# Low weight parts and row arithmetic of a two-layer encoder trunk moved from GpSimd to VectorE

## The chip, the cores and the metric

The kernel runs on one core of a Trainium2 chip. A core has five engines that work beside each other, each through its own queue in order: TensorE (PE: matmuls, and PEld: its weight loads), VectorE (DVE), ScalarE (ACT), GpSimd (POOL) and SyncE (SP, which only issues DMAs here). GpSimd and ScalarE issue some DMAs too. The metric is the device time of one launch in microseconds (us).

## The reference, cut to what matters

The input is 1024 rows of 1024 features; 16 learned rows are put in front, so 1040 rows run through two layers, and the last 1024 come out.

```
def hybrid_mixer(h, ...):                       # h: normalised rows
    proj = h @ w_in
    qkv, z, b_raw, a_raw, sc_b, sc_c, sc_h = split(proj)
    qkv = silu(depthwise_conv_centred(qkv, conv_qkv_w))
    q, k, v = split(qkv); q = l2norm(q); k = l2norm(k)
    ...
    o_fwd = chunk_gated_delta_rule(q, k, v, g[0], beta[0])
    o_bwd = flip(chunk_gated_delta_rule(flip(q), flip(k), flip(v), flip(g[1]), flip(beta[1])))
    o = o_fwd + o_bwd
    o = o * rsqrt(mean(o * o) + RMS_EPS) * dn_norm_w * silu(z)
    y_sc = sc_b * depthwise_conv_centred(sc_c * sc_h, sc_conv_w)
    return concatenate([o, y_sc]) @ w_out

for l in range(2):
    h = h + hybrid_mixer(rmsnorm(h, norm1_w[l]), ...)
    h = h + (silu(gate) * up) @ w_down          # gate, up = split(rmsnorm(h, norm2_w[l]) @ w_gate_up)
return rmsnorm(h, final_norm_w)[16:]
```

Four heads of width 128 go through the gated delta rule, in chunks, forwards and backwards; four groups of 128 channels go through the short gated convolution (sc). All is float32.

## The kernel before, in words

**Precision.** Activations lie transposed: features on the 128 partitions, the 1040 rows along the free dimension. Each float32 matrix is split into a high part, rounded to the matmul's format, and a low part, the rest; a product is three matmuls: high by high (line 157), high by low of the activations (158), low of the weights by high (159). So each 128x512 block of weights that arrives needs a DMA (129), a rounding copy on ACT (130, `whi`) and a subtraction (131, `wlo`). That is `wsplit`, called by `wload`, which gives a tile of weights in two such blocks. `whi` and `wlo` have three buffers each. The flag `lov` chooses the engine of the subtraction: DVE where it is set (the input projection's tiles from the fifth to the end of v, and the first two tiles of the list below), GpSimd elsewhere: the first four tiles of the layer, the rest of the mixer's weights, `w_out`, and the last layer's last weights (`last_weights`). The feed-forward's own weights go through another function (lines 997 and 998), with ACT and DVE.

**Mixer of a layer.** The input projection runs tile by tile, 128 output features each: `dense` does the matmuls of a chunk of rows into a PSUM bank and reads it out on DVE (line 296 by `rstd`, 720 by a row, 905 added to the residual). First k and q (with convolution, lengths, and the chunk matrices, lines 449 to 461), then a substitution of 31 steps for each direction on DVE (lines 523 and 525), then v; then a list of eight tiles: four of z (`z_tile`) and four groups of the short convolution (`sc_tile`). `z_tile` takes silu on ACT and scales the row by a column of `dn_norm_w` (line 671). `sc_tile` takes three projections: the first is multiplied by `rstd` again (716), the second by that at its read-out (720), then the convolution (309, 310), and the product with the third (729; for the last group 732 and a read-out).

**Scan and end of the mixer.** The chunks' scan (`scan_step`) runs forwards and backwards side by side; its steps alternate between PE, ACT and DVE (lines 792 to 845), and dense matmuls of z, sc and of the sc half of `w_out` are set between them. The second direction that reaches a chunk calls `finalize`: it loads the other direction's output `od` (856), subtracts `qs` (857), adds the PSUM result (858), takes the norm (864 to 868), transposes and multiplies by silu(z) (871). Then `O` is split into parts for the output projection (928 high on ACT, 929 low): 16 pieces, of which the pieces of the first quarter of the rows are on DVE and the other 12 on GpSimd. `out_part(0, m)` and then `out_part(1, m)` do the attention half of the output projection for the inner and the outer quarters of the rows, eight tiles each, and behind them the operands of the feed-forward are made (178, 950, 965, 977, 1078), the hand-off to it.

**Feed-forward and end.** Gate, up and down projections run with combined operands (lines 1015 to 1017 and 1435 to 1437). At the end the rows are scaled and stored by `scaled` (1465) on DVE or GpSimd.

**Order.** The order on each queue isn't written out: a scheduler places instructions by priority (`tc.cur_priority`, set by `at_prio`) and by an estimate of when each can run, and then each engine goes through its list. A change of one operation's engine can so move others. In the changed kernel as built, GpSimd's list has 135 rows where it had 318, VectorE's 2910 where it had 2725 (equal neighbours taken together), and the three other lists hold the same work in partly another order.

GpSimd also issues DMAs (`qdma`): the lengths of k and q (412, 415, 608, 611, 612), and it makes the 4-partition inverse of the first 16 rows (474, 475).

Of the kernel before, what the change touches and what calls it, by code (L numbers as in the profile page):

```python
# [7 lines left out]
F32 = mybir.dt.float32  # L8
# [3 lines left out]
ALU = mybir.AluOpType  # L12
# [5 lines left out]
L = 1040  # L18
# [12 lines left out]
P_N1, P_N2, P_CV, P_SC, P_DN = 0, 8, 16, 52, 64  # L31
# [11 lines left out]
def trunk(ctx: ExitStack, tc: tile.TileContext, xT, w_in, w_ba, w_out, w_gu, w_dn,  # L43
          par_d, alog_d, dtb_d, cst_d, eye_d, out):
    nc = tc.nc
# [6 lines left out]
    def nm(p):  # L52
        cnt[0] += 1
        return f"{p}_{cnt[0]}"
# [16 lines left out]
    def pa():  # L71
        return bank("a")
# [27 lines left out]
    tt = nc.vector.tensor_tensor  # L100
    stt = nc.vector.scalar_tensor_tensor
    ts = nc.vector.tensor_scalar
    ptt = nc.gpsimd.tensor_tensor
# [18 lines left out]
    lov = [False]  # L122

    def wsplit(src, hi, lo, raw=None):

        kk = src.shape[1]
        if raw is None:
            raw = wp.tile([128, WK, 128], F32, tag="raw", bufs=2, name=nm("raw"))
        dma(raw[:, 0:kk, :], src)
        whi_done[0] = act(out=hi, in_=raw[:, 0:kk, :], func=AF.Copy)  # L130
        (tt if lov[0] else ptt)(out=lo, in0=raw[:, 0:kk, :], in1=hi.bitcast(F32), op=ALU.subtract)  # L131

    def wload(src, nk):

# [145 lines left out]
    for l in range(DEPTH):  # L280
        last = l == DEPTH - 1
        X, Y = S[l % 2], S[1 - l % 2]
        pcol = lambda c: par[:, l * P_L + c:l * P_L + c + 1]
        rstd = ss
        base = tc.cur_priority

        o0 = 16 if last else 0
# [339 lines left out]
        for pos, i in enumerate(seq):  # L627
# [5 lines left out]
            t = trow()  # L633
# [32 lines left out]
        def z_tile(m):  # L666
            t = trow()
            inproj(12 + m, to_row(t), chunks=ochunks)
            t = t[:, o0:L]
            act(out=t, in_=t, func=AF.Silu)  # L670
            nc.gpsimd.tensor_scalar(out=t, in0=t, scalar1=pcol(P_DN), scalar2=1.0, op0=ALU.mult, op1=ALU.mult)
            dma(szd[m][:, o0:L], t)


# [28 lines left out]
        for i in range(4):  # L703
            t = trow()
# [8 lines left out]
        def sc_tile(i):  # L713
            t0 = trow()
            inproj(16 + 3 * i, to_row(t0))
            ptt(out=t0, in0=t0, in1=rstd, op=ALU.mult)

            def times(t):
                def f(ps, n0, n1):
                    tt(out=t[:, n0:n1], in0=ps, in1=t[:, n0:n1], op=ALU.mult)  # L720
                return f

            inproj(17 + 3 * i, times(t0))
            t2 = trow()
            conv(t0, t2, P_SC + 3 * i)
            if i < 3:
                t1 = trow()
                inproj(18 + 3 * i, to_row(t1), chunks=ochunks)
                ptt(out=t2[:, o0:L], in0=t2[:, o0:L], in1=t1[:, o0:L], op=ALU.mult)
                dma(yd[i][:, o0:L], t2[:, o0:L])  # L730
            else:
                ptt(out=t2, in0=t2, in1=rstd, op=ALU.mult)
                inproj(18 + 3 * i, times(t2), chunks=ochunks)
            return t2

# [20 lines left out]
        O = QT  # L756
# [92 lines left out]
        def finalize(c, n, s0, pof, qs, sz):  # L849

            ob = fin[:, 512 * (nfin[0] % 2):512 * (nfin[0] % 2) + 512]
            nfin[0] += 1
            o = ob[0:n].rearrange("p (h e) -> p h e", h=4)
            dma(sz, szd[:, :, s0:s0 + n].rearrange("m p t -> p m t"))
            if c > 0:
                dma(ob[0:n], od[c])
                ptt(out=o, in0=o, in1=qs[0:n], op=ALU.subtract)
                tt(out=ob[0:n], in0=pof, in1=ob[0:n], op=ALU.add)
            else:
                tt(out=ob[0:n], in0=pof, in1=qs[0:n].rearrange("p h e -> p (h e)"), op=ALU.subtract)  # L860
            pt = v4(pa())
            st = sb.tile([128, 4], F32, tag="st", bufs=2, name=nm("st"))
            for h in range(H):
                act(out=pt[0:n, h, :], in_=o[:, h, :], func=AF.Square, accum_out=st[0:n, h:h + 1])
            stt(out=st[0:n], in0=st[0:n], scalar=1.0 / HD, in1=g[0:n, 0, c, :], op0=ALU.mult, op1=ALU.add)
            act(out=st[0:n], in_=st[0:n], func=AF.Sqrt)
            nc.vector.reciprocal(out=st[0:n], in_=st[0:n])
            tt(out=o, in0=o, in1=st[0:n].unsqueeze(2).to_broadcast([n, 4, 128]), op=ALU.mult)
            for h in range(H):
                nc.tensor.transpose(pt[:, h, 0:n], o[:, h, :], ident[0:n, 0:n])  # L870
            tt(out=O[:, :, s0:s0 + n], in0=pt[:, :, 0:n], in1=sz, op=ALU.mult)
# [17 lines left out]
        t0 = o0  # L889
        yh = big(X[0][2], F32R)  # L890
        ys, yt = [], []
        for i in range(4):
            t = trow() if i < 2 else hb[1][:, i, :] if i < 3 else y3
# [26 lines left out]
        oh, ol = (sb.tile([128, 4, L], F32R, tag=f"P{d}", name=nm("o")) for d in range(2))  # L920
# [5 lines left out]
        for (n0, n1) in hcut[0] + hcut[1]:  # L926
            for h in range(H):
                act(out=oh[:, h, n0:n1], in_=O[:, h, n0:n1], func=AF.Copy)
                (tt if n0 == o0 else ptt)(out=ol[:, h, n0:n1], in0=O[:, h, n0:n1], in1=oh[:, h, n0:n1].bitcast(F32), op=ALU.subtract)
        os_ = [(oh[:, h, :], ol[:, h, :]) for h in range(H)]  # L930

        def half(ap, z):
# [478 lines left out]
        for u, (p, b, m) in enumerate(UNITS):  # L1411
# [16 lines left out]
            for j in range(NJ):  # L1428
# [9 lines left out]
                if b == NBK - 1:  # L1438
                    dh, z, op = TO[p]
                    h = part(hr[4 * dh + m], z, j)  # L1440
# [10 lines left out]
        else:  # L1451
# [22 lines left out]
            for (n0, n1) in FIN:  # L1474
# [8 lines left out]
                for m in range(KT):  # L1483
                    h = hr[m][:, n0:n1]
# [93 lines left out]
```

## Time and profile before

| | |
|---|---|
| median of 3 runs | 2513.88 us (2511.24 to 2517.37) |
| the profiled execution | 2517.22 us |
| its span, first to last instruction | 2515.4 us |
| granted TensorE clock, mean | 0.997 |
| busy: PE, DVE, ACT, POOL | 2478.2, 1696.9, 1045.9, 340.0 us |

How to read the profile's lines. In the page, each engine has its busy time, share of the span and number of instructions; the strips show the span in 40 slices, each digit a busy share in tenths. A row of a group is: source line, engine, operation, output<-inputs, shapes and count, then busy time in us and the mean of one in ns, then the engine's idle time before these instructions and what ended most of it. A row of waits is: who waits, for whom, total us, times, longest. A row of a stretch is: from:to, its length, busy time of PE, PEld, DVE, ACT and POOL with counts, granted clock, DMA share, GB/s. A row of the timeline is: start, duration, engine, line, operation, and in brackets the idle time before it and what ended it. The name `a`, `b`, `a3f` and the like are those of shared buffers.

### The profile page before, as it was taken

How to read it: one execution, taken by the hardware profiler on the slowest of the kernel's cores; microseconds unless marked ns; L12 is line 12 of the kernel's file. 1: busy time of each engine (PE TensorE's matmuls, PEld its weight loads, DVE VectorE, ACT ScalarE, POOL GpSimd, SP SyncE). 2: the span in 40 equal slices, each digit the busy share in tenths (PEclk: the TensorE clock that was granted, in tenths of full speed). 3: DMA queues.
4: the chain of work that ended last, by engine and by line, in shares of the span. 5: the costliest groups of instructions: out<-in, count | busy, mean ns of one | idle time of the engine just before them, and what ended most of it. 6: DMA issues, size and time to landing. Idle time of an engine off the chain costs nothing. (4 is left out here: it accounts for less than half of the span.)

```text
span 2515.4 us, 44862 instructions
## 1 busy us (share of the span) xinstructions
PE 2478.2 (99%) x17508; PEld 2276.9 (91%) x17508; DVE 1696.9 (67%) x3073; ACT 1045.9 (42%) x1944; POOL 340.0 (14%) x359
## 2 busy tenths in 40 slices
PE   8999999999999999999999999999999999999998
PEld 6989999999999999999999888998977888887887
DVE  4788333649877777877657893336698777677765
ACT  5554333535333333344445543335453333234444
POOL 1031212331000000000111212133400000000012
PEclk9999999999999999999999999999999999999999
DMA  3444353624323332764224443446332233238541
GB/s 127 135 166 149 112 161 130 212 77 136 116 102 102 108 102 81 256 198 133 92 77 145 152 154 116 143 131 205 120 126 101 97 105 117 90 112 279 177 120 68
DMA packets 199530, 335.27 MB, mean 133 GB/s; under 512 B 23404, under 2 KB 85668, under 8 KB 199316
## 3 DMA queue, kind: packets, MB, share of 16 engines
q1 hardware_dynamic: 171204, 293.84, 35.3%
q10 hardware_dynamic: 25936, 34.19, 4.2%
q0 software_dynamic: 2176, 4.36, 0.6%
q8 instruction: 138, 2.26, 0.4%
q14 instruction: 76, 0.62, 0.1%
HBM read 250.31 MB, written 81.99 MB: 132 GB/s over the span
## 5 line engine op out<-in xcount | busy, mean ns | idle before, releaser
L131 POOL TENSOR_TENSOR wlo<-raw,whi 128x512 fp32r<-128x512 f32 x132 | 176.4, 1338 | 1285.4 <-ACT whi L130 1116.7
L157 PE MATMUL pacc<-a,whi 128*128 128x346 f32 (+1 forms) x808 | 263.6, 329 | 8.8 <-ACT whi L130 7.6
L159 PE MATMUL pacc<-a,wlo 128*128 128x346 f32 (+1 forms) x808 | 262.4, 326 | 0.7 <-DVE wlo L131 0.5
L157 PE MATMUL pacc<-b,whi 128*128 128x346 f32 (+2 forms) x672 | 234.0, 349 | 2.4 <-ACT b L900 1.8
L159 PE MATMUL pacc<-b,wlo 128*128 128x346 f32 (+2 forms) x672 | 233.1, 348 | 0.8 <-DVE wlo L131 0.8
L158 PE MATMUL pacc<-a,whi 128*128 128x346 f32 (+1 forms) x688 | 225.1, 327 | 0.0
L130 ACT ACTIVATE whi<-raw 128x512 fp32r<-128x512 f32 x168 | 106.0, 631 | 228.3 <-PE pacc L158 124.9
L158 PE MATMUL pacc<-b,whi 128*128 128x346 f32 (+2 forms) x580 | 200.8, 346 | 0.0
L157 PEld LDWEIGHTS pacc<-a,whi 128*128 128x128 f32 x808 | 152.2, 189 | 14.6 <-ACT whi L130 8.1
L159 PEld LDWEIGHTS pacc<-a,wlo 128*128 128x128 f32 x808 | 152.9, 189 | 1.7 <-DVE wlo L131 0.8
L157 PEld LDWEIGHTS pacc<-b,whi 128*128 128x128 f32 x672 | 126.9, 189 | 14.5 <-issue 3.1
L159 PEld LDWEIGHTS pacc<-b,wlo 128*128 128x128 f32 x672 | 126.6, 189 | 9.8 <-DVE wlo L131 1.1
L158 PEld LDWEIGHTS pacc<-a,whi 128*128 128x128 f32 x688 | 130.3, 189 | 2.6 <-issue 2.1
L997 ACT ACTIVATE whi<-rw 128x512 fp32r<-128x512 f32 x92 | 57.6, 631 | 140.1 <-PE pf L1016 36.4
L158 PEld LDWEIGHTS pacc<-b,whi 128*128 128x128 f32 x580 | 109.5, 189 | 6.9 <-issue 0.4
L997 ACT ACTIVATE b<-rw 128x512 fp32r<-128x512 f32 x64 | 39.9, 631 | 135.0 <-PE pacc L1016 37.4
L296 DVE TENSOR_TENSOR a<-pacc,rstd 128x346 f32<-128x346 f32 (+2 forms) x59 | 32.7, 555 | 89.6 <-PE pacc L159 89.5
L296 DVE TENSOR_TENSOR b<-pacc,rstd 128x346 f32<-128x346 f32 (+1 forms) x63 | 32.5, 516 | 82.8 <-PE pacc L159 82.8
L131 POOL TENSOR_TENSOR a<-raw,a 128x512 fp32r<-128x512 f32 x3 | 3.9, 1285 | 597.1 <-ACT a L130 597.1
L997 ACT ACTIVATE a<-rw 128x512 fp32r<-128x512 f32 x64 | 40.0, 629 | 101.7 <-PE pacc L1016 60.3
L998 DVE TENSOR_TENSOR wlo<-rw,whi 128x512 fp32r<-128x512 f32 x92 | 62.8, 686 | 4.8 <-ACT whi L997 4.1
L1015 PE MATMUL pacc<-b,whi 128*128 128x260 f32 (+1 forms) x172 | 53.5, 311 | 0.7 <-ACT b L1051 0.7
(966 smaller groups left out, 8012.8 us busy)
## 6 DMA issues: line engine op xcount, KB each, us to landing
raw<-in_w_in SPq DMA_DIRECT2D x112, 256.0 KB, 2.5
raw<-in_w_gu SPq DMA_DIRECT2D x104, 256.0 KB, 2.9
rw<-in_w_gu SPq DMA_DIRECT2D x88, 256.0 KB, 3.0
rw<-in_w_dn SPq DMA_DIRECT2D x94, 192.0 KB, 2.7
rec<-vkd SPq DMA_DIRECT2D x61, 256.0 KB, 2.7
raw<-in_w_out SPq DMA_DIRECT2D x48, 256.0 KB, 2.8
b<-ad SPq DMA_DIRECT2D x45, 260.0 KB, 3.3
a<-ad SPq DMA_DIRECT2D x45, 256.0 KB, 5.2
```

Of the source, the lines that this page charges most:

```text
L130: whi_done[0] = act(out=hi, in_=raw[:, 0:kk, :], func=AF.Copy)
L131: (tt if lov[0] else ptt)(out=lo, in0=raw[:, 0:kk, :], in1=hi.bitcast(F32), op=ALU.subtract)
L157: mm(ps[:, :n], wh, xh[:, n0:n1], start=(k == 0), stop=False)
L158: mm(ps[:, :n], wh, xl[:, n0:n1], start=False, stop=False)
L159: mm(ps[:, :n], wl, xh[:, n0:n1], start=False, stop=(k == K - 1))
L296: tt(out=t[:, n0:n1], in0=ps, in1=rstd[:, n0:n1], op=ALU.mult)
L997: act(out=hi, in_=src, func=AF.Copy)
L998: tt(out=lo, in0=src, in1=hi.bitcast(F32), op=ALU.subtract)
L1015: mm(ps[:, :CW], w[0][:, k, :], th[:, cs], start=first and k == 0, stop=False, skip_group_check=True)
```

## The change

The low weight parts (131), the scaling of z (671), the row products of the short convolution (716, 729, 732), the subtraction in `finalize` (857) and the low parts of `O` (929) all go to VectorE. GpSimd keeps its DMA issues, the 4-partition inverse and its share of the last products (1465).

```
@@ wsplit
-        (tt if lov[0] else ptt)(out=lo, in0=raw[:, 0:kk, :], in1=hi.bitcast(F32), op=ALU.subtract)
+        tt(out=lo, in0=raw[:, 0:kk, :], in1=hi.bitcast(F32), op=ALU.subtract)
@@ z_tile
-            nc.gpsimd.tensor_scalar(out=t, in0=t, scalar1=pcol(P_DN), scalar2=1.0, op0=ALU.mult, op1=ALU.mult)
+            ts(out=t, in0=t, scalar1=pcol(P_DN), scalar2=None, op0=ALU.mult)
@@ sc_tile
-            ptt(out=t0, in0=t0, in1=rstd, op=ALU.mult)
+            tt(out=t0, in0=t0, in1=rstd, op=ALU.mult)
...
-                ptt(out=t2[:, o0:L], in0=t2[:, o0:L], in1=t1[:, o0:L], op=ALU.mult)
+                tt(out=t2[:, o0:L], in0=t2[:, o0:L], in1=t1[:, o0:L], op=ALU.mult)
...
-                ptt(out=t2, in0=t2, in1=rstd, op=ALU.mult)
+                tt(out=t2, in0=t2, in1=rstd, op=ALU.mult)
@@ finalize
-                ptt(out=o, in0=o, in1=qs[0:n], op=ALU.subtract)
+                tt(out=o, in0=o, in1=qs[0:n], op=ALU.subtract)
@@ low parts of O
-                (tt if n0 == o0 else ptt)(out=ol[:, h, n0:n1], in0=O[:, h, n0:n1], in1=oh[:, h, n0:n1].bitcast(F32), op=ALU.subtract)
+                tt(out=ol[:, h, n0:n1], in0=O[:, h, n0:n1], in1=oh[:, h, n0:n1].bitcast(F32), op=ALU.subtract)
```

## The prediction

> **What bounds the kernel now.** I read the page first: the engines' busy shares and the strips of 40 slices.
>
> ```profile
> span 2515.4 us, 44862 instructions
> ...
> PE 2478.2 (99%) x17508; PEld 2276.9 (91%) x17508; DVE 1696.9 (67%) x3073; ACT 1045.9 (42%) x1944; POOL 340.0 (14%) x359
> ...
> DVE  4788333649877777877657893336698777677765
> POOL 1031212331000000000111212133400000000012
> ```
>
> TensorE (PE) is busy for 2478.2 us of 2515.4. All that any change of VectorE (DVE) and GpSimd (POOL) work can give back is the 37.2 us in which PE idles. The strips say where the two engines meet: POOL has work in slices 0 to 9 and 19 to 28 (the mixers of the two layers) and at the very end, and DVE there runs from 3 tenths (slices 4 to 6) to 9.
>
> The waits come next, first those of all engines and then those of PE.
>
> ```profile
> POOL wlo L131 <- ACT whi L130: 1116.7, 98, 614.6
> ...
> ACT whi L130 <- PE pacc L158: 124.9, 59, 8.6
> ```
>
> ```profile
> PE pacc L157 <- ACT whi L130: 8.7, 5, 5.9
> ...
> PE pacc L159 <- DVE wlo L131: 1.4, 2, 0.8
> ```
>
> Columns: total us, times, longest. POOL waits for ScalarE (ACT), ACT waits for PE to release the weight buffers, and PE waits for a low weight part only twice, 1.4 us together, both of them parts that DVE makes already. No low part made by POOL is waited for: POOL's slowness as such is hidden.
>
> Last, busy time in the stretches that matter (PE, PEld, DVE, ACT, POOL in this order):
>
> ```profile
> 0.00:10.00 10.00, 2.88 (x7) 1.99 (x8) 3.14 (x7) 5.46 (x8) 2.70 (x6) 1.00 0.77 247
> 90.00:260.00 170.00, 166.62 (x1461) 159.15 (x1460) 147.98 (x313) 87.56 (x117) 41.47 (x88) 1.00 0.53 174
> 260.00:450.00 190.00, 190.00 (x1684) 186.73 (x1683) 60.19 (x153) 67.94 (x173) 44.14 (x31) 1.00 0.40 130
> 577.00:615.00 38.00, 35.27 (x289) 34.60 (x288) 36.78 (x56) 20.91 (x37) 6.35 (x5) 1.00 0.39 127
> 1350.00:1530.00 180.00, 177.67 (x1464) 162.85 (x1463) 153.79 (x309) 87.86 (x116) 33.31 (x60) 1.00 0.51 168
> 1720.00:1740.00 20.00, 17.95 (x92) 15.04 (x92) 14.30 (x25) 12.77 (x40) 7.36 (x5) 0.91 0.75 269
> 1740.00:1800.00 60.00, 60.00 (x341) 51.79 (x340) 29.82 (x62) 21.98 (x73) 23.97 (x25) 1.00 0.33 110
> 1800.00:1823.00 23.00, 23.00 (x196) 23.00 (x195) 18.26 (x34) 14.33 (x23) 11.10 (x9) 1.00 0.56 186
> 1823.00:1860.00 37.00, 34.20 (x210) 29.26 (x209) 36.34 (x55) 20.34 (x32) 6.17 (x4) 0.95 0.38 124
> 2500.00:2515.40 15.40, 6.89 (x68) 6.22 (x67) 6.86 (x15) 5.21 (x13) 7.52 (x10) 0.83 0.41 138
> ```
>
> PE's idle time: 7.1 us in the first 10, 8.5 after 2500; of the 21.6 left, 3.4 and 2.3 lie in the stretches of substitution (90 to 260, 1350 to 1530), 2.1 in 1720 to 1740, and 2.7 and 2.8 in the two hand-offs from mixer to feed-forward (577 to 615, 1823 to 1860), where DVE is 97 and 98% busy. Those hand-offs are DVE's; the scan (260 to 450, and to 1800 in the second layer) has DVE half idle.
>
> **What moves.** These groups of POOL work go to DVE; the rows are line, operation, shape, count | busy, mean ns.
>
> ```profile
> L131 POOL TENSOR_TENSOR wlo<-raw,whi 128x512 fp32r<-128x512 f32 x132 | 176.4, 1338 | 1285.4 <-ACT whi L130 1116.7 <-PE pacc L158 41.9 <-DMA raw<-in_w_in 38.8
> ...
> L857 POOL TENSOR_TENSOR b3f<-b3f,qs 128x512 f32<-128x512 f32 x8 | 10.3, 1296 | 39.1 <-DMA b3f<-od 24.6 <-ACT pa L864 6.9 <-PE pacc L158 5.7
> L716 POOL TENSOR_TENSOR b<-b,rstd 128x1040 f32<-128x1040 f32 x4 | 9.8, 2439 | 4.8 <-DVE b L296 3.3 <-PE pb L485 1.5
> ...
> L929 POOL TENSOR_TENSOR o<-b,o 128x260 fp32r<-128x260 f32 x12 | 9.6, 832 | 6.7 <-PE pb L807 6.7
> ```
>
> And this is what such shapes cost on DVE, and what DVE pays now when POOL runs beside it:
>
> ```profile
> L131 DVE TENSOR_TENSOR wlo<-raw,whi 128x512 fp32r<-128x512 f32 x36 | 24.7, 686 | 1.9 <-ACT whi L130 1.6
> ...
> L1356 DVE TENSOR_TENSOR a<-a,rstd 128x1040 f32<-128x1040 f32 x21 | 26.1, 1241 | 0.6
> ...
> L178 DVE SCALAR_TENSOR_TENSOR b<-a,par,b 128x346 fp32r<-128x346 f32 x14 | 12.2, 873 | 4.9 <-ACT b L177 4.9
> ...
> L865 DVE SCALAR_TENSOR_TENSOR st<-st,g 128x4 f32<-128x4 f32 x16 | 9.6, 601 | 13.8 <-ACT pa L864 13.7
> ...
> L868 DVE TENSOR_TENSOR b3f<-b3f,st 128x512 f32<-128x512 f32 x8 | 7.7, 966 | 0.2
> ...
> L178 DVE SCALAR_TENSOR_TENSOR b<-a,par,b 128x348 fp32r<-128x348 f32 x7 | 4.1, 581 | 2.5 <-ACT b L177 2.5
> ...
> L867 DVE RECIPROCAL st<-st 128x4 f32<-128x4 f32 x16 | 2.8, 173 | 2.3 <-ACT st L866 2.3
> ```
>
> Added to DVE: 140 low weight parts (the 132 and the eight of the last weights) at 0.686 are 96.0 us; 16 subtractions L857 of the same width 11.0; 16 row products (L716 x8, L729 x6, L732 x2) at 1.241 are 19.9; 8 scalings L671, at most the 1.241 of a product of that width, 9.9; 24 splits L929 of about 260 columns, at 0.43, halfway between L867's 0.173 and L131's 0.686, 10.3. Together 147 us, which would put DVE at 1844 us, 73% of the span.
>
> Taken from DVE: what POOL costs it today. Operations of one shape differ there: L178 of 346 columns takes 873 ns and of 348 columns 581, and L865 on four elements a partition takes 601 where L867 takes 173. Three groups alone give (873-581)x14 = 4.1, (601-173)x16 = 6.8 and, against L131's 686, (966-686)x8 = 2.2: 13 us at least. These are instructions with both tensors in SBUF that met a POOL instruction.
>
> **What lies on the path**, against the profiled execution's own 2517.2 us (span 2515.4 and 1.8 around it), which is 3.3 above the median of the three runs:
>
> 1. *Start, line 131.* The first low parts are made after 5.9 us on POOL (1.3 each, 0.69 on DVE), in a stretch that waits for loads. In the changed program as built the first two stand on DVE's queue ahead of two L178 splits, so what they gain the splits may wait. Between -1.3 and +0.7; I take -0.6.
>
> 2. *Third product and hand-off inside the mixer, lines 732, 857, 131.* The second layer shows it:
>
> ```profile
> 1723.36 2.92 POOL L732 TENSOR_TENSOR a<-a,rstd 128x1040 f32<-128x1040 f32 x1 [3.11 <-DVE st L867]
> 1726.32 0.69 DVE L720 TENSOR_TENSOR a<-pacc,a 128x512 f32<-128x512 f32 x1 [2.29 <-POOL a L732]
> ...
> 1729.61 1.29 POOL L857 TENSOR_TENSOR a3f<-a3f,qs 128x512 f32<-128x512 f32 x1 [3.33 <-DMA a3f<-od]
> 1730.86 2.94 POOL L131 TENSOR_TENSOR wlo<-raw,whi 128x512 fp32r<-128x512 f32 x2
> 1730.94 1.74 DVE L1290 TENSOR_TENSOR rw<-rw,rw 128x512 f32<-128x512 f32 x1 [3.33 <-POOL a3f L857]
> 1732.60 1.22 DVE L865 SCALAR_TENSOR_TENSOR st<-st,g 128x4 f32<-128x4 f32 x1
> ...
> 1734.62 0.50 PE L157 MATMUL pacc<-b,whi 128*128 128x512 f32 x1 [1.80 <-ACT b L900]
> ```
>
> L732 falls from 2.92 to 1.24 before the L720 that waits for it, L857 from 1.29 to 0.69, L1290 and L865 lose about 1.05 each: 4.4 us out of a chain at whose end PE idles 2.05 in this stretch (1.80 of it in this row). What is late next is the load of od, which no step shortens; on DVE the waiting L857 now holds the queue, and behind it stand the PSUM read-outs L720. Between -2.05 and +3.3 (that wait once more, in front of DVE); I take -1.5. The first layer's L732 has no wait of PE behind it: 0.
>
> 3. *The two hand-offs, lines 131 and 929.* Five and four low parts fall into stretches where DVE is full: +3.4 and +2.7. Against it POOL's 6.35 and 6.17 us there no longer get in DVE's way, at most that much. So between -5.5 (PE's whole idle time there) and +6.1; the low parts are certain and the relief is not, so I take +2.
>
> 4. *Rest of the mixers.* With PE at 190 of 190 us in the first layer's scan and DVE at 60, 44 us of POOL work become about 23 of DVE: the queue in front of a PSUM read-out or a scan step grows by one instruction, 0.7 to 1.2, and PE has other work in line. Zero; without that cover, each of its 16 steps would cost 0.7, 11 us. In the two stretches of substitution DVE goes from 87 and 85% to a little more; if PE's 5.7 us of waits there grow in step they cost +2; between -5.7 and +5.7. I take +2.
>
> 5. *Queues.* GpSimd's own issues (L412, L415, L608 to L612) lose the arithmetic ahead of them, and wait for DVE as before: 0. The last-weight parts at 2439 to 2451 are eight of 0.69 in a window with PE at 100%: 0, and 5.5 if it were bare. The last products (L1465) stay on POOL.
>
> Sum: -0.6 - 1.5 + 2 + 2 = +1.9. That is 2519.1 by this execution's own time and 2515.8 by the median of the runs, 2516. A difference under 0.2%, 5 us, is about what a measurement of this kernel can tell from none; the forecast is no change.
>
> **Rivals.** *Slower: the last chunk of the second layer comes too late.* The output projection's second half needs it at 1816.3, and it is ready at 1800.0:
>
> ```profile
> 1789.42 0.69 DVE L858 TENSOR_TENSOR a3f<-pb,a3f 128x512 f32<-128x512 f32 x1 [2.01 <-PE pb L828]
> ...
> 1796.03 0.69 DVE L871 TENSOR_TENSOR a<-pa,rec 128x512 f32<-128x512 f32 x1 [0.93 <-PE pa L870]
> ...
> 1799.27 0.74 DVE L929 TENSOR_TENSOR o<-a,o 128x256 fp32r<-128x256 f32 x2
> ```
>
> ```profile
> 1816.27 0.28 PE L157 MATMUL pf<-o,whi 128*128 128x256 f32 x1
> ```
>
> From L858 to L871 it takes 6.6 us now, with six instructions from the one to the next; in the changed program 31 instructions stand between, among them six low parts, 25 more at about 0.5, some 12 us. If DVE, to which 24 us of POOL work in 1740 to 1800 bring about 12, falls behind by that much as well, the chunk is 24 late against a slack of 16.3: 8 us of idle PE, and the hand-off after it pays its 2.7 and the first layer's 3.4 without relief: +14, 2528. It decides from 16 us of lateness on. For it speaks how full DVE is from 1800 (18.3 of 23 us, with nine more low parts of 0.69 to come); against it, that DVE has 30 of 60 us free just before. A rule of the Trainium skill stands on its side: Perfetto Trace Analysis, section Optimizing Scalar/DVE Operations, says that where DVE is saturated, moving work off it, even to GpSimd, may make sense; the change does the reverse. The same passage doubts that offload between these two helps, since they share an SBUF read port.
>
> *Faster: the relief of DVE is worth more than the work it takes on.* If each POOL instruction stopped DVE for its length, L865's 601 ns against 173 being the case in point, the hand-offs give their 5.5 us, the stretch at 1720 its 2.05, and a quarter of the substitutions' 5.7 goes, 1.4: -9, which is 2505 by the median's measure. Against it: PE's longest wait of all, 8.7 us for L157, names ACT and not DVE. The Trainium skill's page SBUF — State Buffer, section Who interferes with whom, states this as a rule: a DVE instruction with two SBUF inputs contends with a GpSimd instruction that reads SBUF, and the loser is blocked fully. The trace agrees in L865 and L1290 (1.74 against 0.69); by the rule alone the move would be a gain.
>
> *It does nothing because POOL was idle cover anyway* is the forecast itself.
>
> **Chances.** Forecast 0.44 (of it 0.38 within 0.2%, 0.04 slower, 0.02 faster); late chunk 0.33 (0.32 slower, 0.01 same); relief 0.23 (0.20 faster, 0.03 same). So faster 0.22, same 0.42, slower 0.36. The forecast's own range is 2510 to 2521. The bounds of the steps, both ways, reach from -14.6 to +15.8 (2499 to 2530 by the median); the range that holds eight in ten goes from the faster rival to just past the slower one: 2505 to 2531.
>
> **What would show it.** Right: DVE near 1830 us busy and POOL near 65; L865 and L868 at one mean near 170 and 690 ns; PE's idle total near 37 us, with the wait at 1734 gone and those at 605 and 1850 as long or longer. Wrong towards slower: PE waits for L928 or L929 at the start of the projection's second half in the second layer, or DVE idle in front of L857 until od lands, with L720 or L905 behind it. Wrong towards faster: DVE falls below 90% in the hand-offs and PE's idle time there vanishes.

## The result and the profile after

The changed kernel takes 2508.96 us (median of 19 runs, 2504.89 to 2511.97) where the kernel before takes 2516.28 on the same chips (19 runs, 2511.24 to 2518.01). The ratio is 0.9972, 95% interval 0.9965 to 0.9978: 7 us faster, just beyond the 0.2% that a measurement can tell. The prediction's range held the time; its forecast, no change, did not come about.

The page of the changed kernel, its span, busy times and the strips of VectorE (DVE) and GpSimd (POOL):

```profile
span 2507.1 us, 44757 instructions
...
PE 2473.1 (99%) x17508; PEld 2273.7 (91%) x17508; DVE 1776.3 (71%) x3277; ACT 1049.2 (42%) x1946; POOL 67.0 (3%) x155
...
DVE  5788445769877777877657884356798777678774
POOL 0040000000000000000000200000000000000002
```

The span is 8.3 us shorter than before. TensorE (PE) idles for 34.0 us of it, 3.2 less than before, and is busy for 5.1 us less with the same 17508 matmuls: in this pair of executions most of the difference is not idle time. A good part of it is the granted clock, which had more low stretches in this one execution of before; over many executions the clock makes far less of a difference (last section). VectorE took over work that cost GpSimd some 270 us, and is busy for only 79 us more.

The same stretches as in the prediction (columns as there), of the changed kernel:

```profile
0.00:10.00 10.00, 2.93 (x8) 2.23 (x9) 3.43 (x9) 5.35 (x8) 0.21 (x4) 1.00 0.77 241
90.00:260.00 170.00, 164.47 (x1449) 157.26 (x1448) 145.09 (x321) 87.15 (x116) 29.79 (x80) 1.00 0.54 175
577.00:615.00 38.00, 37.97 (x313) 37.43 (x312) 37.02 (x63) 23.55 (x41) 0.00 (x0) 1.00 0.41 131
1350.00:1530.00 180.00, 177.38 (x1459) 162.22 (x1458) 152.43 (x314) 86.39 (x114) 17.05 (x46) 1.00 0.50 165
1720.00:1740.00 20.00, 20.00 (x118) 17.36 (x117) 14.57 (x31) 12.29 (x37) 0.00 (x0) 1.00 0.84 309
1740.00:1800.00 60.00, 60.00 (x354) 52.43 (x353) 39.11 (x83) 24.36 (x77) 0.00 (x0) 1.00 0.34 111
1800.00:1823.00 23.00, 23.00 (x197) 23.00 (x196) 22.70 (x48) 14.07 (x26) 0.00 (x0) 1.00 0.57 184
1823.00:1860.00 37.00, 34.44 (x192) 27.89 (x191) 36.87 (x56) 23.51 (x37) 0.00 (x0) 1.00 0.39 131
```

A stretch of fixed times holds somewhat later work in the faster kernel. In the first hand-off (577 to 615) PE works through, 37.97 of 38 us against 35.27 before; so it does in 1720 to 1740. The substitution of the first layer (90 to 260) got worse, 164.47 against 166.62. Beside this stands the clock: the row of 1823 to 1860 has 1.00 where it had 0.95, that of 1720 to 1740 1.00 where it had 0.91.

PE's longest waits in the changed kernel:

```profile
PE pacc L157 <- ACT whi L130: 7.1, 3, 5.9
PE pa L424 <- ACT kt L426: 4.1, 3, 3.2
PE pf L1435 <- ACT a L1196: 4.0, 1, 4.0
```

The wait of L424 for `kt`, 1.5 us before, is 4.1 now; its longest part, 3.2 us at 146.5, stands where PE loses in the first layer.

And the groups on VectorE, in separate forms:

```profile
L131 DVE TENSOR_TENSOR wlo<-raw,whi 128x512 fp32r<-128x512 f32 x168 | 115.3, 688 | 69.4 <-ACT whi L130 62.3 <-PE pf L807 6.3 <-DMA rec<-vkd 0.2
...
L178 DVE SCALAR_TENSOR_TENSOR b<-a,par,b 128x346 fp32r<-128x346 f32 x14 | 8.1, 577 | 2.1 <-ACT b L177 2.0
...
L857 DVE TENSOR_TENSOR b3f<-b3f,qs 128x512 f32<-128x512 f32 x8 | 5.5, 691 | 12.9 <-DMA b3f<-od 10.9 <-ACT vv L810 2.0
...
L868 DVE TENSOR_TENSOR b3f<-b3f,st 128x512 f32<-128x512 f32 x8 | 5.5, 690 | 0.2
...
L865 DVE SCALAR_TENSOR_TENSOR st<-st,g 128x4 f32<-128x4 f32 x16 | 2.5, 155 | 0.2 <-ACT pa L864 0.2
```

L865 falls from 601 to 155 ns, L868 from 966 to 690, L178 of 346 columns from 873 to 577.

To see where time goes along the program, I took the moment at which PE has done the same amount of matmul work in two traces, and the difference of these moments (worked out from the start of every matmul). By stretch of the kernel before, in us against it, from one profiled execution each. In the ten traces of kernels whose start is as before, the first stretch lies between -1.9 and +0.7, so a difference of 1 us or so says nothing:

| kernel | 0–53 start | 53–252 k, q, substitution | 252–545 scan | 545–645 hand-off | 645–1715 | 1715–1792 end of 2nd mixer | 1792–1905 hand-off | rest |
|---|---|---|---|---|---|---|---|---|
| changed kernel | -1.3 | +1.8 | +0.2 | -2.3 | -0.5 | -4.4 | -2.9 | +1.1 |
| only the hand-offs' work moved | -1.6 | -0.5 | +0.3 | -2.4 | -0.6 | -3.1 | -4.1 | +0.9 |
| all low parts moved but the hand-offs' | -1.8 | +3.8 | +1.9 | +1.5 | -0.6 | -1.3 | +0.2 | -1.0 |

The gain lies in the two hand-offs and in the end of the second mixer. Of the changed kernel's -2.3, -4.4 and -2.9 there, less idle time of PE makes 2.2, 2.1 and 1.2, and 1.7 each of the last two is a stretch of lower clock that the execution of before had and this one had not. The last two rows are experiments, below.

### The profile page after: what moved, and what is told of

It reads as the page before. It is cut to its first block, busy times and chain, and to the rows that moved or that the text cites. A ratio compares the mean times of both kernels' runs of the same rounds, so it can differ in the third digit from the quotient of the medians.

```text
span 2507.1 us, 44757 instructions
## 1 busy us (share of the span) xinstructions
PE 2473.1 (99%) x17508; PEld 2273.7 (91%) x17508; DVE 1776.3 (71%) x3277; ACT 1049.2 (42%) x1946; POOL 67.0 (3%) x155
## 5 line engine op out<-in xcount | busy, mean ns | idle before, releaser
L131 DVE TENSOR_TENSOR wlo<-raw,whi 128x512 fp32r<-128x512 f32 x168 | 115.3, 688 | 69.4 <-ACT whi L130 62.3
L1017 PE MATMUL pacc<-b,wlo 128*128 128x260 f32 (+1 forms) x172 | 52.6, 306 | 0.0
```

What stands on the lines that cost most here:

```text
L131: tt(out=lo, in0=raw[:, 0:kk, :], in1=hi.bitcast(F32), op=ALU.subtract)
L1017: mm(ps[:, :CW], w[1][:, k, :], th[:, cs], start=False, stop=stop and k == nk - 1, skip_group_check=True)
```

## The experiments

Theories, formed on the two traces. **A, contention:** GpSimd's reads of SBUF hold up VectorE's instructions with two inputs in SBUF, VectorE is what the hand-offs wait for, and so its relief is the gain. **B, latency:** moved instructions that stand on the path (L732, L857, L929, the low parts) are shorter on VectorE, and give buffers back earlier. **C, order:** the scheduler made a luckier order. The trace of before has a case for A in the first hand-off (timeline; start, duration):

```profile
587.62 1.30 POOL L131 TENSOR_TENSOR wlo<-raw,whi 128x512 fp32r<-128x512 f32 x1 [4.73 <-DVE wlo L998]
...
587.82 1.65 DVE L950 TENSOR_TENSOR rstd<-rstd,sq 128x520 f32<-128x520 f32 x1
```

The same square sum in the changed kernel, with the low part beside it on VectorE:

```profile
588.16 0.69 DVE L950 TENSOR_TENSOR rstd<-rstd,sq 128x520 f32<-128x520 f32 x1
588.77 0.68 DVE L131 TENSOR_TENSOR wlo<-raw,whi 128x512 fp32r<-128x512 f32 x1
```

The sum started 0.20 us behind a GpSimd instruction of 1.30 and took 1.65 instead of 0.69. Doing GpSimd's work itself costs VectorE 0.68; being held up by it cost 0.96.

### Parts of the change alone

*Low weight parts alone*

```
@@ wsplit (all else as before)
-        (tt if lov[0] else ptt)(out=lo, in0=raw[:, 0:kk, :], in1=hi.bitcast(F32), op=ALU.subtract)
+        tt(out=lo, in0=raw[:, 0:kk, :], in1=hi.bitcast(F32), op=ALU.subtract)
```

> Only the low parts of the weights (L131) go to VectorE, every other operation stays on GpSimd. Theory A (contention: GpSimd's reads of SBUF hold up VectorE's instructions with two inputs in SBUF, and the hand-offs and the wait at 1734 us pay for it): L131 is 176 of the some 240 us that left GpSimd, so most of the gain of 7.3 us should be here, 2510 to 2512 us, with the mean of L865 near 200 ns. Theory B (latency: the gain is the shorter duration of the few moved instructions that stand on the path, L732, L857 and L929): little is gained, 2513 to 2517 us, and TensorE still idles at about 1734 us for the 2.05 us wait.

Measured: 2507.16 us beside 2514.95, ratio 0.9969 (0.9958 to 0.9981). One line of the seven gives the whole gain, more than A expected (it is 187 of the 273 us that left GpSimd, which I had put at 240). PE still waited about 1734, a little (18.54 us busy of 20 in 1720 to 1740), so B's path of L732 is not what decides.

*Row work alone*

```
@@ z_tile, sc_tile (all else as before)
-            ptt(out=t0, in0=t0, in1=rstd, op=ALU.mult)
+            tt(out=t0, in0=t0, in1=rstd, op=ALU.mult)
... (likewise lines 671, 729, 732)
```

> Only the four row operations (L671, L716, L729, L732) go to VectorE. Theory A: some 43 of 240 us of GpSimd's work go, so about a fifth of the gain, 2513 to 2517 us, and the hand-off stretches stay as before (37 us idle of TensorE altogether). Theory B: the wait at 1734 us and the lower clock after it go, which by the progress of TensorE is worth 5 us: 2510 to 2512 us, with 20 us of TensorE busy in the stretch 1720:1740.

Measured: 2516.57 us, ratio 1.0007 (0.9998 to 1.0016). B's sign came, 19.72 us of PE in 1720 to 1740 and 3.5 us won between 1715 and 1792, but not its gain: the hand-offs lost 2.9 and 4.9 us in the same trace, which comes from the slowest of its eleven executions (2521.07).

*The hand-offs' work alone, and its complement*

```
@@ before, w_out's weights and the split of O
-            dense(wload(w_out[l, m, :, 4:8, :], 4), ys, chunks, add_h(m))
+            lov[0] = True; dense(wload(w_out[l, m, :, 4:8, :], 4), ys, chunks, add_h(m)); lov[0] = False
...
-                (tt if n0 == o0 else ptt)(out=ol[:, h, n0:n1], ...)
+                tt(out=ol[:, h, n0:n1], ...)
...
-            dense(wload(w_out[l, m, :, 0:4, :], 4), os_, hcut[z], add_h(m), pwide)
+            lov[0] = True; dense(wload(w_out[l, m, :, 0:4, :], 4), os_, hcut[z], add_h(m), pwide); lov[0] = False
```

> The kernel before with only the work of the hand-offs on VectorE: the 48 low parts of the output projection's weights (L131 called from L918 and L942) and the low parts of the attention rows (L929). Theory A1 (the relief that pays lies in the two hand-offs from mixer to feed-forward): nearly the whole gain, 2507 to 2510 us beside before at 2515, TensorE busy at least 37.4 us in 577:615, L865 near 200 ns or less. Theory A2 (the gain is spread over the whole kernel, wherever GpSimd worked): a gain in proportion to the 48 of 132 low parts, about 2 to 3 us, 2512 to 2514 us.

The complement sets `lov[0] = 2` in the two `w_out` lines, and line 131 takes `(ptt if lov[0] == 2 else tt)`; lines 671 to 929 stay as before.

> The complement: the low parts of all weights on VectorE (as in the run with the low parts alone, 2507 us) but those of the output projection, 48 of them, which are on GpSimd; the row work on GpSimd. Theory A1: no gain, 2513 to 2517 us, 35.3 us of TensorE in 577:615, and L865 at 550 to 600 ns. Theory A2: two thirds of the gain, 2509 to 2511 us.

Measured: 2506.03 us, ratio 0.9963 (0.9950 to 0.9977), and 2519.04 us, 1.0011 (1.0002 to 1.0020), both beside 2515.47. Stretches of the first (577 and 1823), then of the second:

```profile
577.00:615.00 38.00, 37.70 (x309) 36.98 (x307) 38.00 (x63) 25.38 (x43) 0.00 (x0) 1.00 0.40 132
...
1823.00:1860.00 37.00, 35.27 (x189) 28.42 (x188) 36.94 (x57) 23.12 (x36) 0.00 (x0) 1.00 0.35 124
```

```profile
90.00:260.00 170.00, 164.00 (x1437) 156.77 (x1436) 144.39 (x315) 86.83 (x115) 34.86 (x83) 0.99 0.52 170
577.00:615.00 38.00, 35.77 (x283) 35.34 (x282) 35.67 (x57) 20.77 (x36) 8.44 (x6) 0.96 0.44 144
...
1823.00:1860.00 37.00, 33.49 (x216) 29.90 (x215) 34.04 (x54) 19.85 (x31) 7.65 (x5) 0.95 0.39 133
```

The gain lies wholly in the hand-offs' work; the other 92 low parts bring a loss of some 3 us, in the first layer's substitution (164.00 us of PE against 166.62 before). By the medians the first is the best kernel of all, 2 to 3 us under the changed one; its interval and that of the changed kernel overlap, so the two are not told apart.

*Which part of the hand-offs' work*

The 32 low parts of line 942 alone, then L929 alone, each otherwise as before:

```
-            dense(wload(w_out[l, m, :, 0:4, :], 4), os_, hcut[z], add_h(m), pwide)
+            lov[0] = True; dense(wload(w_out[l, m, :, 0:4, :], 4), os_, hcut[z], add_h(m), pwide); lov[0] = False
```

> The kernel before with only the 32 low parts of the output projection's attention half (L131 called from L942) on VectorE; the 16 of L918 and the 24 of L929 stay on GpSimd. By the progress of TensorE in the run with all of the hand-offs' work, 3 us of the 9 are gained before 1746 us of the second layer, where only L918's parts lie, and 6 us in the two hand-offs: so 2509 to 2511 us if L942's parts carry the hand-offs; 2514 to 2517 us if L929 does.

```
-                (tt if n0 == o0 else ptt)(out=ol[:, h, n0:n1], ...)
+                tt(out=ol[:, h, n0:n1], ...)
```

> The kernel before with only the low parts of the attention rows (L929) on VectorE. If they carry the hand-offs, 2509 to 2511 us; if the weights' low parts do, 2514 to 2517 us, since 24 instructions of 0.79 us on GpSimd become 24 of 0.42 us on VectorE and 10 us more of VectorE stand in stretches where it is full.

Measured beside 2515.96: 2508.56 us, ratio 0.9970 (0.9958 to 0.9982), and 2516.57 us, ratio 1.0000 (0.9990 to 1.0010). Thirty-two instructions carry most of it; L929 carries nothing.

*Without the rows; without GpSimd at the end*

```
@@ the changed kernel, sc_tile and z_tile
-            tt(out=t0, in0=t0, in1=rstd, op=ALU.mult)
+            ptt(out=t0, in0=t0, in1=rstd, op=ALU.mult)
... (likewise lines 671, 729, 732)
```

> All low parts (L131, L929) and the subtraction of the last chunks (L857) on VectorE, the scalings and products of rows (L671, L716, L729, L732) left on GpSimd. The row work alone measured +1.6 us [-0.5, +4.0] on VectorE. If that cost holds beside the low parts, this is the best of all, 2504 to 2507 us; if the rows' effect is nothing once the low parts are away, it is as the changed kernel, 2507 to 2510 us; if L732's wait at 1734 us decides, it is slower than the changed kernel by 2 to 3 us, 2510 to 2513 us.

```
@@ scaled, of the changed kernel
-   mul=tt if n0 == 16 and q > 5 else ptt
+   mul=tt
...
-                mul, by = (ptt, sv) if q in (3, 6) else (tt, pb)
+                mul, by = tt, pb
```

> The changed kernel with the 16 output products of L1465 that GpSimd still does on VectorE too. Theory A, contention at the end: their 1.06 us each hold up VectorE's L189 and L905 in the last stage, so 1 to 2 us less than the changed kernel, 2506 to 2508 us. Rival: the two last products of GpSimd stand beside VectorE's six at the very end, and without them VectorE does eight in a row, two times 0.35 us more, while the earlier fourteen are covered: 0.5 to 1 us more, 2509 to 2510 us.

Measured beside 2515.47: 2508.55 us, 0.9971 (0.9960 to 0.9981): the rows count for nothing beside the low parts. And 2511.65 us, 0.9984 (0.9974 to 0.9994): outside both expectations. By the medians the last products are better left on GpSimd, by some 3 us, but this interval and that of the changed kernel (0.9965 to 0.9978) overlap, so it isn't shown.

### Reads put back, orders held

*Over the whole kernel.* In both runs all instructions of PE, VectorE, ScalarE (ACT) and of SyncE's queue stand in exactly the order of the changed kernel; by theory C alone they would be as fast.

```
@@ the changed kernel, wsplit (and likewise 2 to 5 behind each other moved instruction)
+    extra = lambda n, prev: [after(ptt(out=dum, in0=ones[:, 0:96], in1=ones[:, 32:128], op=ALU.subtract), prev) for _ in range(n)]
...
+        extra(0 if lov[0] else 3, whi_done[0])
@@ the control
+    extra = lambda n, prev: [after(nc.gpsimd.memset(dum, 0.0), prev) for _ in range(n)]
```

> The changed kernel, with extra GpSimd work whose result nobody reads: behind each instruction that was moved stand two to five subtractions of 128x96 (ones minus ones, both in SBUF), about the duration that GpSimd had there before. The orders of TensorE, VectorE, ScalarE and the SyncE queue are exactly those of the changed kernel. Theory A: VectorE is held up again, its busy time returns from 1776 to 1830-1845 us, L865 returns to 500-600 ns, and the time returns to that of before, 2514 to 2518 us. Theory B and theory C (the scheduler's other order of instructions makes the gain): nothing waits for the extra work, so 2507 to 2511 us.

> The same extra GpSimd instructions in the same places, as fills of 128x96 with zero, which read nothing from SBUF. It is the control of the run with subtractions. Theory A, if the reads make the contention: as the changed kernel, 2507 to 2511 us, VectorE busy 1775 to 1785 us, L865 at 155 to 175 ns. If any GpSimd instruction on SBUF holds up VectorE, it lies with the run with subtractions, 2514 to 2518 us. Theories B and C: 2507 to 2511 us.

Measured beside 2514.95: with reads 2522.08 us, ratio 1.0029 (1.0019 to 1.0039); with fills 2510.69 us, 0.9977 (0.9968 to 0.9986). The pages, reads first:

```profile
PE 2480.5 (98%) x17508; PEld 2276.4 (90%) x17508; DVE 1801.3 (71%) x3277; ACT 1049.8 (42%) x1946; POOL 399.0 (16%) x783
```

```profile
PE 2474.8 (99%) x17508; PEld 2275.3 (91%) x17508; DVE 1775.6 (71%) x3277; ACT 1048.8 (42%) x1946; POOL 179.3 (7%) x783
```

783 instructions of GpSimd each; the ones that read cost 11 us and lengthen VectorE's work by 26 us, the ones that only write do neither. That is the rule of the Trainium skill, SBUF — State Buffer, section Who interferes with whom: a VectorE instruction with two SBUF inputs contends with a GpSimd instruction that reads SBUF, not with one that only writes. The fills are also shorter, 0.18 us against 0.53, but what lengthens the same 3277 instructions of VectorE is the reads. C alone does not keep the gain where GpSimd reads so much; that the order has no part in it is not shown. My sizes were off both ways. VectorE came to 1801 us (1830 to 1845 expected), and L865 stayed at 190 ns (500 to 600 expected): reads of 96 columns hold VectorE up less than those of 512 (L950 takes 758 and 778 ns here, 984 with the long reads below). And the time rose past that of before: against the changed kernel the run with reads lost 4 us in the first layer's scan, 2 in the first hand-off and 9 in the second, where it had far more reading than before:

```profile
1823.00:1860.00 37.00, 32.06 (x204) 27.31 (x203) 36.80 (x57) 19.88 (x31) 33.49 (x45) 1.00 0.38 128
```

That is 33.49 us of GpSimd against 6.17 before.

*In the hand-offs only.* On the kernel with only the hand-offs' work on VectorE, two subtractions behind each of its 48 low parts and 24 splits, orders held again; then the fills; then subtractions released by the low part instead of ScalarE's copy.

```
+        extra(2 if lov[0] == 2 else 0, whi_done[0])
...
+                extra(0 if n0 == o0 else 2, tt(out=ol[:, h, n0:n1], ...))
```

> The kernel with only the hand-offs' work on VectorE (2506 us), with two subtractions of 128x96 on GpSimd, read by nobody, behind each of the 48 low parts of the output projection and behind each of the 24 low parts of the attention rows that GpSimd had. At 0.53 us each (332 us more of busy GpSimd for 628 of them, in the earlier run with subtractions) that is 76 us, beside the 83 us that GpSimd had there before. The orders of the other engines are those of the kernel without them. Theory A (contention in the hand-offs): the gain is lost, 2512 to 2518 us, VectorE's busy time up by 5 to 15 us. Rival B (the way through GpSimd is longer: a low part takes 1.3 us there in place of 0.69, and stands behind others in its queue): nothing waits for the extra work, so 2504 to 2508 us.

> The same extra instructions as fills, which read nothing: 0.18 us each. Theory A and rival B: 2504 to 2508 us. If any work of GpSimd there costs (its writes, or the waits that it carries), 2510 to 2515 us.

```
-        extra(2 if lov[0] == 2 else 0, whi_done[0])
+        extra(2 if lov[0] == 2 else 0, low_)        # low_: VectorE's subtraction
```

> As the run with two subtractions behind each low part of the hand-offs, but released by the low part itself (VectorE's subtraction) and not by ScalarE's copy ahead of it, so that in the second hand-off, too, GpSimd reads while the hand-off's work runs: some 5 us of busy GpSimd in 577:615 and in 1823:1860 (6.4 and 6.2 us before). Orders on the other engines unchanged. Theory A: the rest of the gain goes too, 2512 to 2517 us, with TensorE busy 35 to 36.5 us in 577:615. If the second hand-off's gain is from the shorter way of the low parts, the time stays at 2508 to 2511 us and TensorE keeps its gain of some 4 us between 1800 and 1870.

Measured: 2510.70 us, ratio 0.9976 (0.9967 to 0.9986), and 2506.24 us, 0.9966 (0.9953 to 0.9978), both beside 2515.96; then 2508.91 us beside 2516.47, 0.9973 (0.9962 to 0.9983). The first hand-off with reads, then with fills:

```profile
577.00:615.00 38.00, 36.13 (x287) 35.70 (x286) 37.16 (x61) 21.69 (x39) 6.42 (x8) 0.96 0.38 126
```

```profile
577.00:615.00 38.00, 38.00 (x316) 37.65 (x314) 37.17 (x65) 23.59 (x41) 1.79 (x10) 1.00 0.42 139
```

With 6.42 us of reading GpSimd, 6.35 before, PE idles for 1.87 us of the first hand-off (2.73 before), and a stretch of lower clock, 0.96, takes the rest of its gain; fills leave all of it. But the third run read for as long there and lost little:

```profile
577.00:615.00 38.00, 37.47 (x307) 36.74 (x306) 38.00 (x63) 24.32 (x42) 6.22 (x8) 1.00 0.40 128
```

So the amount of reading does not set the cost by itself; it was released by another instruction, and met other work. In the second hand-off the first run read for only 2.7 us and kept its gain, and the third, with 3.7 us, kept it too, at 2508.91 us: what was expected if that gain comes from the shorter way of the low parts. The reads took back 2 to 4.5 us of the 9 by the medians, and the intervals overlap: part of the gain at most, not all of it.

### Reads and buffers apart

GpSimd's low part also held the weights' raw buffer, one of two, until it was done. From the end of ScalarE's copy to the end of the last reader, the traces give means of 1.44 and 1.75 us in the two hand-offs before, and of 1.01 and 1.28 us with the hand-offs' work moved. These runs hold it, with and without reading:

```
@@ the kernel with only the hand-offs' work on VectorE, behind line 131
+        lov[0] == 2 and ptt(out=raw[:, 0:kk, :], in0=raw[:, 0:kk, :], in1=hi.bitcast(F32), op=ALU.subtract)
@@ the control; then the same with range(1)
+        [nc.gpsimd.memset(raw[:, 0:kk, :], 0.0) for _ in range(3) if lov[0] == 2]
```

> The kernel with only the hand-offs' work on VectorE (2506 us); behind each of the 48 low parts of the output projection GpSimd does the same subtraction once more into the raw buffer, read by nobody: 128x512 with two inputs, 1.34 us, and the raw buffer is held until it is done, as before. Theory A (contention): VectorE's instructions wait behind these long reads as before, and the gain goes, 2513 to 2518 us. Theory B' (the buffer is held longer): 2511 to 2516 us here too, and as much in the next run.

> The control: in the same places three fills of the raw buffer with zero, 0.53 us each, so the buffer is held 1.6 us, longer than by the subtraction, but nothing is read. The scheduler puts 139 of some 14000 rows of TensorE otherwise than in the run with the subtraction. Theory A: 2505 to 2509 us. Theory B': 2511 to 2517 us, as the run with the subtraction or more.

> As the run with three fills, with one fill of 0.53 us behind each low part of the output projection: the raw buffer is free some 1.5 us after the end of ScalarE's copy, as before (1.44 us and 1.75 us in the two hand-offs), and GpSimd reads nothing. 140 of some 14000 rows of TensorE stand otherwise than in the kernel with only the hand-offs' work on VectorE. Theory A (contention alone): 2505 to 2509 us, ScalarE's wait for VectorE's L905 in 560:640 at 2 to 4 us (8.0 before). Theory B' (the time for which the buffer is held): 2511 to 2516 us, and new waits of ScalarE for the loads in the hand-offs.

| behind each low part | held for (two hand-offs) | time, beside before | ratio |
|---|---|---|---|
| subtraction of 128x512 | 3.37, 3.35 us | 2533.01, 2516.51 | 1.0070 (1.0057 to 1.0083) |
| three fills | 2.84, 2.84 us | 2517.62, 2516.51 | 1.0007 (0.9998 to 1.0016) |
| one fill | 1.81, 2.10 us | 2511.29, 2515.97 | 0.9984 (0.9975 to 0.9993) |
| nothing | 1.01, 1.28 us | 2506.03, 2515.47 | 0.9963 (0.9950 to 0.9977) |

With fills B' had the better numbers: one fill lies in its range, three just above it, and theory A's 2505 to 2509 us did not come. With the long reads neither had. They cost 15 us over fills in the same places, and hold the buffer only 0.5 us longer; VectorE's groups in 577 to 615 show what the reads do, first with subtractions, then with three fills:

```profile
L950 DVE TENSOR_TENSOR rstd<-rstd,sq 128x520 f32<-128x520 f32 x7 | 6.9, 984 | 0.0
L977 DVE SCALAR_TENSOR_TENSOR a<-a,par,a 128x520 f32<-128x520 f32 x7 | 6.8, 988 | 0.0
```

```profile
L977 DVE SCALAR_TENSOR_TENSOR a<-a,par,a 128x520 f32<-128x520 f32 x8 | 5.9, 747 | 0.0
L950 DVE TENSOR_TENSOR rstd<-rstd,sq 128x520 f32<-128x520 f32 x7 | 4.8, 689 | 0.0
```

But holding the buffer seems to cost as well, with nothing read: 5 us by the medians at 1.8 to 2.1 us (the intervals just overlap), the whole gain at 2.8. The order is not held here: against the kernel with only the hand-offs' work moved, 237 of PE's 17508 matmuls stand at another place with one fill, and 1976 with three. ScalarE's waits in 560 to 640 (us, times, longest) show what the buffer does. Before:

```profile
ACT sq L949 <- DVE a L905: 8.0, 10, 2.4
...
ACT whi L130 <- DMA raw<-in_w_out: 1.0, 1, 1.0
```

With three fills:

```profile
ACT whi L130 <- DMA raw<-in_w_out: 10.6, 9, 2.2
ACT sq L949 <- DVE a L905: 2.4, 3, 1.4
```

With subtractions it waits 15.2 us for L905 and 2.5 for loads. Before, ScalarE waited for a late VectorE and hardly for loads, which looks like contention; with only the hand-offs' work moved the wait for L905 is 2.6 us. L905 itself, with one input in PSUM, is not held up (0.42 us in both traces); it is late because those ahead of it in VectorE's queue were. But this is no sure mark of contention. With one fill, where GpSimd reads nothing, the waits are close to those of before, and theory A had expected 2 to 4 us for L905:

```profile
ACT sq L949 <- DVE a L905: 5.3, 9, 2.3
...
ACT whi L130 <- DMA raw<-in_w_out: 1.2, 1, 1.2
```

What stays open: how the 9 us divide. That GpSimd's reads cost time is shown, by reads and fills in held orders. That this made the gain is shown in part. The run with one fill says that not all of it is the buffers': it held them longer than before did, GpSimd read nothing in the hand-offs, and it was still 4 us faster than before (0.9975 to 0.9993). On a straight line through nothing, one fill and three fills, some 6.5 us of time for each us of holding, before's 1.44 and 1.75 us would be worth some 3 of the 9 us; this is an estimate, as the order differs between those runs. The order is the rival that no run settles: the kernel with only the hand-offs' work moved has 2356 matmuls at another place than before.

## Why the prediction was wrong

It was the rival *faster* that came, with a chance of 0.23; its mechanism was named, and the likeliest case gave it too little weight. That its 9 us lie near the measured 7 is in part luck: it counted 1.4 us of gain in the substitutions, where the first layer's lost 1.8, and nothing for the clock.

- **The relief, "13 us at least", was mis-sized.** What moved costs, at the changed kernel's means, 143 us (140 low parts x 0.688, 16 subtractions x 0.69, 16 products x 1.24, 8 scalings x 0.75, 24 splits x 0.42). The durations of all VectorE instructions add up to 1862.5 us in the trace of before and 1960.0 in that of the changed kernel, 97.5 more, so 46 us were given back, three and a half times the three groups that I had added up. Three groups of over four hundred are a floor, and I used the floor as the size. Busy time rose by less, from 1696.9 to 1776.3, since it counts once what one instruction overlaps with the next (588.16 + 0.69 against 588.77 above). So 1830 was too high for a second reason, by 18 us: I had added durations to a busy time.
- **Step 3, the hand-offs, is the step that failed.** "The low parts are certain and the relief is not, so I take +2": measured -2.3 and -2.9. The step put the work that VectorE takes on above the waiting that it is spared, without a size for the second; in the whole kernel it was spared 46 us, and PE's idle time in the two hand-offs fell by 2.2 and 1.2 us instead of growing. The held-up L950 above shows why its own price was wrong: 0.68 of work added took away 0.96 of blocking. The sum, -5.2, lies near the step's end of -5.5, but that end was PE's idle time alone, and 1.7 us of what was measured are the lower clock. How much of the rest is relief and how much the buffers' earlier release is open (above).
- **Step 2, the third product, came with the right sign and too small.** -1.5, bounded at -2.05 by PE's idle time; measured -4.4. The bound was wrong: PE's 2.05 us of idle time went, and with it 1.7 us of lower clock behind it, which another execution may not have (last section). Nor is L732's length the only cure. The row work alone won 3.5 us there, the hand-offs' work alone 3.1 with L732 still on GpSimd.
- **Step 1** said -0.6; the -1.3 measured is within what traces with the same start differ by. **Step 4** came at +1.8 in the first layer's substitution and -0.5 over the stretch that holds the second's, against +2 together. This cost is real: the seven traces with the other low parts on VectorE lose 1.8 to 4.7 us between 53 and 252 (1.1 to 2.3 without the lower clock that six of them have there), the ten without lie between -2.4 and +1.4, and the complement run as a whole is slower. **Step 5** said 0; the end is 1.1 us later, as it is (+0.9) with only the hand-offs' work moved.
- **"All that any change can give back is the 37.2 us in which PE idles" was false.** Of the 8.3 us between the two profiled spans, 3.2 came from idle time and 5.1 from busy time, of which 2.4 by the granted clock.
- **The rival *slower* was there and cost nothing.** Its two rows and the split behind them, in the timeline of the changed kernel:

```profile
1791.01 0.68 DVE L858 TENSOR_TENSOR a3f<-pb,a3f 128x512 f32<-128x512 f32 x1
...
1807.09 0.69 DVE L871 TENSOR_TENSOR a<-pa,rec 128x512 f32<-128x512 f32 x1
...
1811.56 0.42 DVE L929 TENSOR_TENSOR o<-a,o 128x256 fp32r<-128x256 f32 x1
```

  From L858 to L871 it takes 16.1 us where it took 6.6; I had added 12. But PE is busy for 23.00 of 23 us from 1800 to 1823: the slack took it.

Of the signs to watch, L865 and L868 came at one mean (155 and 690 ns), POOL came at 67.0 us, the wait at 1734 went, but that at 605 went too, and VectorE did stand idle in front of L857 until `od` landed (10.9 us in the row above), at no cost to PE. The sign set for *faster* came by half. PE's idle time vanished in the first hand-off only (37.97 of 38 us busy, 34.44 of 37 in the second), and VectorE did not fall below 90%: it is busy for 37.02 of 38 us and 36.87 of 37. It is as full as before and gets further, 63 instructions in the first where it did 56.

## What to carry to other kernels

Before work is moved between VectorE and GpSimd, compare one shape's duration where GpSimd reads beside it and where it doesn't, over all groups, and set the whole difference against the work, durations against durations; if a stretch is bound by a VectorE that GpSimd holds up, helping it from GpSimd can cost more than it takes off. Then move only what runs in that stretch: here 32 of the some 200 moved instructions made most of the gain, and 92 other low parts, moved without them, cost 3 us. And a control that only writes, in held orders, tells contention from much else that a moved instruction changes; the buffers that it holds need a control of their own.

## What the runs showed of the hardware

**A short wait of PE can be paid twice.** The granted clock in two slices of 10 us, of before and then of the changed kernel:

```profile
1730.00:1740.00 10.00, 7.95 (x38) 6.52 (x37) 9.03 (x14) 6.92 (x19) 3.79 (x3) 0.83 1.02 394
1850.00:1860.00 10.00, 9.12 (x37) 6.49 (x38) 9.96 (x14) 6.35 (x11) 0.00 (x0) 0.83 0.29 97
```

```profile
1730.00:1740.00 10.00, 10.00 (x61) 8.68 (x60) 9.80 (x22) 6.61 (x19) 0.00 (x0) 1.00 1.03 389
1850.00:1860.00 10.00, 8.83 (x38) 6.72 (x37) 9.99 (x13) 6.27 (x10) 0.00 (x0) 1.00 0.50 154
```

PE's matmuls behind the wait of 1.80 us at 1734, in the timeline of before:

```profile
1737.11 0.63 PE L157 MATMUL pacc<-b,whi 128*128 128x512 f32 x1
1737.54 0.63 PE L158 MATMUL pacc<-b,whi 128*128 128x512 f32 x1
...
1739.50 0.39 PE L159 MATMUL pacc<-b,wlo 128*128 128x512 f32 x1
1739.73 0.39 PE L157 MATMUL pacc<-b,whi 128*128 128x512 f32 x1
```

They start 0.43 us apart, and 0.23 from 1739 on. A slice of 10 us at 0.83 is 1.7 us of work lost, two of them 3.4; the changed kernel's execution lost 1.0 us more at its end. The Trainium skill, TensorE: Matmul & The Clock Gate, section HAM oscillation — how this bites in real kernels, gives idle gaps of more than about 3.4 us as what lowers the clock; here waits of 1.80 and 1.62 us stood ahead of such slices. It isn't every wait: before's 1.73 us at 605 and the changed kernel's 3.2 us at 146 left the clock at 1.00 in their slices. Nor is it the same wait each time: with L929 alone moved, PE waits 1.52 us at the same place, 1734, and the slice has 1.00, but the one at 605 has 0.83. So one trace's clock is in part chance. Over all executions, the mean granted clock is 0.9971 for the changed kernel (19) and 0.9967 for before (111, beside the experiments): about 1 us of the 7, not the 2.4 of the profiled pair.

**Holding a buffer seems to have a steep price.** With the raw buffer held for 2.84 us in place of 1.01 and 1.28, on 48 low parts, the kernel took 11 us longer, with GpSimd reading nothing in the hand-offs; part of that may be the order, which differs too.
